# Splitting weights by chunks of four channel blocks in three 4 KB tiles, instead of by two blocks in six 2 KB tiles

## The chip, the cores and the metric

The kernel runs on one core of a Trainium2 chip. A core has five engines with queues of their own, each working through its instructions in the order in which the program issues them: TensorE (matmuls; PE in the profile, its weight loads PEld), VectorE (DVE), ScalarE (ACT), GpSimd (POOL) and SyncE (SP, which here issues all DMAs). SBUF is the on-chip memory of 128 partitions; a tile of "4 KB" has 4 KB in each partition. Matmuls write to PSUM banks of 128 x 512 float32.

The metric is the time of one execution on the device in microseconds. Three runs of the kernel before gave 1795.52, 1795.69 and 1798.46 us; the median is 1795.69.

## The reference

One layer over 1024 tokens and 2048 channels, in float32:

```python
hn = rmsnorm(h, norm_gain)
proj = hn @ w_in                       # 2048 x 4096
pool_in, pool_gate, ssm_in, ssm_gate = four column blocks of 1024
ya = pool_mixer(pool_in, w_pool, pool_scale) * silu(pool_gate)
yb = ssm_mixer(ssm_in, ...) * silu(ssm_gate)
h = h + concatenate([ya, yb]) @ w_out  # 2048 x 2048
h = h + (p @ w_ple) * sigmoid(h @ w_ple_gate)
return rmsnorm(h, final_gain)
```

`pool_mixer` takes trailing means over windows of 2, 4, 8 and 16 tokens and a 256 x 256 product for each of four channel groups. `ssm_mixer` is a state-space layer: 64 groups of 16 channels share 64 complex states each; its output passes GELU and a gated linear unit with the 1024 x 2048 weight `w_glu`.

## The kernel before, in words

**Products in two parts.** TensorE multiplies a reduced form of float32 (`F32R` in the code). To keep precision, each operand is split into a high part (rounded to that form) and a low part (the rest), and three products are summed: high x high, high x low, low x high. For weights this split is done on the fly, each time a weight chunk arrives: ScalarE writes the high part (`act.copy`, a CAST in the profile, L199), VectorE subtracts it from the raw chunk for the low part (a TENSOR_TENSOR w<-raw,w in the profile; all such operations pass the helper at L96).

**Chunks and steps.** The dense work is a list of `chunks` (weights loaded by one DMA) and a list of `steps` (what TensorE does with a part of a chunk). A chunk of the usual kind is 128 output channels by four channel blocks of 128 (256 KB, tile `raw`, of which there are three, `r_p`). A narrow step takes two channel blocks (`kk` = 0 or 2 of the chunk) for one or both halves of 512 tokens: 2 blocks x 3 products = 6 matmuls of 128 x 512 with one half, 12 with both. Chunks of only two blocks, with one step each, occur in the first stage (steps 0 to 7, 24 to 39 and 56 to 63, when x is still arriving; steps 8 to 23 and 40 to 55 use chunks of four blocks) and in the products of the pooling branch (eight steps in all). There are 568 narrow steps from 304 chunks. Steps 0 to 63 have 6 matmuls each, steps 64 and on have 12 until near 785 us. At the end of the kernel wide steps take one channel block by 512 columns as the moving operand; there are 128 of them with a chunk of their own.

**The split before.** `split(s)` (L189) makes the split weights of one step. A narrow step gets one tile of `w_p` with 2 x 2 x 128 float32 (2 KB): cast and subtraction of 256 columns. A wide step gets two such tiles, one for the high and one for the low part (`split_wide`, L203): cast and subtraction of 512 columns. `w_p` has `NW` = 6 tiles.

**The order.** The order of all engines is written out by hand. `emit(s)` (L245) issues for step s, in this order: loads whose raw tile is free (`emit_loads`, L237: the load of chunk c is issued after the last split of chunk c-3 has been issued), stores held back, then splits of coming steps, as far as step s + `SA` (`SA` = 4) and as long as the steps from s on together hold no more than `NW` tiles (`nw`: one for a narrow step, two for a wide one, L153 and L161); then the `pre` work of the step, the background generators (`bg`), the matmuls (`run_mats`, L210) and the `post` work. So on ScalarE and VectorE the split for step s+4 stands ahead of the other work of step s. A new tile in a place that an old one had waits until all that read the old one are done.

**Work around it.** In the first stage, `x_proc` (L310) turns pieces of x on TensorE, ScalarE copies them out (`xt`, L318) and VectorE splits them (`hn`, L321 and L322); ScalarE also sums squares (L336); `u_raw` (L396) and `u_scale` (L402) work on outputs on VectorE. From step 40 on the state-space branch runs in the background, one piece for each 2.56 us of matmul work counted: `ss_prep`, then `ss_b` and `ss_l` side by side, `ss_v`, `ss_scan`, `ss_y`. `ss_b` (L603) builds a tile `m` in three VectorE operations (L613 to L615) in one piece, and the next piece turns it on TensorE (L621) ahead of that step's matmuls and copies it out on ScalarE (L623). `ss_scan` (L780) is a chain of VectorE operations on 128 x 64 elements with larger ones on GpSimd between; `ss_y` (L805) begins with a mask on GpSimd (`ytm`, L825). The windows of the pooling branch (`pool_win`, L916) run in the background later, on GpSimd, VectorE and ScalarE.

Of the kernel before, what the change touches and what calls it, by code (L numbers as in the profile page):

```python
# [17 lines left out]
L = 1024          # tokens  # L18
HT = 512          # tokens per half
D = 2048  # L20
KD = D // P       # 16 channel blocks of the model
W = 1024          # width of a branch
KW = W // P       # 8 channel blocks of a branch
G = 64            # state-space groups
N = 64            # states of a group
C = 16            # channels of a group
T = 8             # tokens of a chunk of the scan
NC = L // T       # chunks
# [7 lines left out]
NW = 6            # tiles of split weights  # L36
# [3 lines left out]
def hybrid_trunk(ctx: ExitStack, tc: tile.TileContext, x, p, norm_gain, w_in, w_pool, pool_scale,  # L40
# [33 lines left out]
    g_d = dr.tile([W, T, NC], F32, name="g_d")            # t descending  # L74
# [6 lines left out]
    K_d = dr.tile([G * C * P + P], F32, name="K_d")       # overlapping rows, see ss_y  # L81
# [25 lines left out]
    # ------------------------------------------------------------ constants  # L107
# [7 lines left out]
    sgn = cst.tile([P, 2], F32, name="sgn")     # [:,0] -1 | +1, [:,1] +1 | -1  # L115
# [12 lines left out]
    dT = cst.tile([64, 16], F32, name="dT")      # of (four groups, c), by four groups  # L128
    same = cst.tile([64, C], F32, name="same")   # of (g ci), co: ci = co
    parT = cst.tile([P, 24], F32, name="parT")  # L130
    mask = cst.tile([P, T], F32, name="mask")   # of (ci ti), to: ti + to < T
# [9 lines left out]
    # ------------------------------------------------------------ dense steps  # L141
# [3 lines left out]
    def chunk(ap, nk):  # L145
        chunks.append({"ap": ap, "nk": nk, "raw": None, "last": None})
        return len(chunks) - 1

    def step(ch, kk, mats, pre=(), post=()):
        """mats: list of (bank key, activation getters of two channel blocks, start, stop)"""  # L150
        chunks[ch]["last"] = len(steps)
        steps.append({"ch": ch, "kk": kk, "mats": mats, "pre": list(pre), "post": list(post),
                      "w": None, "nw": 1, "dur": 1.28 * len(mats)})  # L153

    def wide_step(ch, mats, post=()):
        """tokens on partitions; mats: list of (bank key, bank pool, activation getter, columns,
        weights or None for those of the chunk, start, stop)"""
        if ch is not None:
            chunks[ch]["last"] = len(steps)
        steps.append({"ch": ch, "kk": None, "mats": mats, "pre": [], "post": list(post),  # L160
                      "w": None, "nw": 0 if ch is None else 2, "dur": 0.64 * len(mats)})  # L161
# [8 lines left out]
    def store(o, i, n=1):  # L170
        """a store on the queue of the loads, held back so that it does not wait there"""
        late.append([n, o, i])
# [16 lines left out]
    def split(s):  # L189
        sd = steps[s]  # L190
        if sd["ch"] is None:
            return
        if sd["kk"] is None:
            raw = chunks[sd["ch"]]["raw"].rearrange("p a c -> p (a c)")
            sd["w"] = split_wide(raw)
            return
        raw = chunks[sd["ch"]]["raw"][:, sd["kk"]:sd["kk"] + 2]
        w = w_p.tile([P, 2, 2, P], F32R, tag="w", name="w")
        act.copy(out=w[:, 0], in_=raw)  # L199
        tt(dve, w[:, 1], raw, f(w[:, 0]), ALU.subtract)  # L200
        sd["w"] = w

    def split_wide(raw):  # L203
        hi, lo = (w_p.tile([P, 2, 2, P], F32R, tag="w", name="w").rearrange(
            "p a b c -> p (a b c)") for _ in range(2))
# [4 lines left out]
    def run_mats(s):  # L210
        sd = steps[s]
        w = sd["w"]
# [14 lines left out]
        for i in range(2):  # L227
            for j, (wi, ai) in enumerate(((0, 0), (0, 1), (1, 0))):
                for key, ks, start, stop in sd["mats"]:
                    a = acts[ks[i]]  # L230
                    pe.matmul(out=banks[key], lhsT=w[:, wi, i], rhs=a[:, ai],  # L231
                              start=start and i == 0 and j == 0, stop=stop and i == 1 and j == 2)

    SA = 4
# [10 lines left out]
    def emit(s):  # L245
        emit_loads()
        emit_stores()
        while (state["split"] <= min(s + SA, len(steps) - 1)
               and sum(d["nw"] for d in steps[s:state["split"] + 1]) <= NW):
# [19 lines left out]
        sd["w"] = None  # L269

    def block(wap, ks, halves, akey, bkey, post):
        """One block of 128 output channels over the given channel blocks and token halves."""
# [1176 lines left out]
```

## Time and profile before

| | |
|---|---|
| three runs, median | 1795.69 us |
| lowest, highest | 1795.52, 1798.46 us |
| span of the profiled execution | 1795.3 us |
| DVE idle before w<-raw,w of 256 columns, waiting for the cast | 333.4 us of 335.6 |
| ACT idle before the cast of 256 columns, waiting for matmuls | 449.8 us of 531.6 |
| HBM read, written | 178.63 MB, 55.05 MB |

The time of the profiled execution as a whole isn't recorded beside its span; the span, from its first to its last instruction, is 0.4 us below the median of the three runs. Busy time of an engine is the time in which one of its instructions ran. In rows of a timeline the first number is the start in microseconds from the start of the span, the second how long the row lasts, "xN" how many instructions of the same kind it merges; in square brackets stand the idle time of the engine ahead of the row and what ended it. In a group of instructions the numbers after the bar are busy time in us, mean ns of one instruction, and idle time of the engine ahead of them. Instructions of one engine overlap at their ends, so from the start of one to the start of the next may be less than the duration. In tables of stretches the bounds are followed by the length, then the busy time of each engine, the granted clock of TensorE (1.00 is full speed), the share of the DMA engines and GB/s.

### The profile page before, as it was taken

The numbers are of one execution on the slowest core, as the hardware profiler recorded it, in microseconds if no ns is written. First come the engines' busy times: TensorE is split into PE (matmuls) and PEld (weight loads), VectorE is DVE, ScalarE is ACT, GpSimd is POOL, SyncE is SP. The second block draws the span as 40 slices with busy tenths as digits, with TensorE's granted clock in tenths as the row PEclk, the third lists the DMA queues.
The fourth block names the chain that finished last, engine by engine and source line by source line (L and its number), as shares of the span: only waits on it lengthen the run. The fifth ranks groups of instructions, "written<-read, shape, count | busy, mean of one in ns | idle before, by whom it ended". The sixth has DMA issues, their size and how long they took to land.

```text
span 1795.3 us, 23117 instructions
## 1 busy us (share of the span) xinstructions
PE 1748.6 (97%) x8054; PEld 1444.8 (80%) x8054; DVE 975.2 (54%) x1792; ACT 613.2 (34%) x1389; POOL 370.3 (21%) x395
## 2 busy tenths in 40 slices
PE   8999899999989999999999999999999999999998
PEld 7888678887768888887888888888888888777787
DVE  5755987479985745447533442222245554466542
ACT  6641355341124522126322231111133333344332
POOL 0065143024341114204011100000001211233320
PEclk9999999999989999999999999999999999999999
DMA  8853333542246622247532353333365333363312
GB/s 264 240 167 94 126 119 125 169 126 71 65 129 188 205 83 82 83 126 191 170 112 76 93 184 106 94 96 98 100 194 194 120 114 124 113 208 117 120 59 94
DMA packets 299510, 235.21 MB, mean 131 GB/s; under 512 B 51689, under 2 KB 242178, under 8 KB 298498
## 3 DMA queue, kind: packets, MB, share of 16 engines
q1 hardware_dynamic: 299394, 233.75, 42.0%
q8 instruction: 63, 1.03, 0.2%
q14 instruction: 53, 0.43, 0.1%
HBM read 178.63 MB, written 55.05 MB: 130 GB/s over the span
## 4 chain that ended last, share of the span: by engine, by line
PE 80%; DVE 10%; issue 3%; POOL 3%; ACT 2%; DMA 1%; SPq 0%; ACTq 0%; POOLq 0%; DVEq 0%
PE mm L231 58%; PE mm L221 16%; DVE w L96 2%; PE aux L221 2%; DVE V L96 2%; POOL nat L96 2%; DVE V L756 1%; ACT V L758 1%; POOL pf L96 1%; PE aux L867 1%; PE bk L1184 1%; PE aux L865 1%; DVE m L96 1%; DVE tB L96 1%; PE aux L316 1%
## 5 line engine op out<-in xcount | busy, mean ns | idle before, releaser
L231 PE MATMUL mm<-hn,w 128*128 128x512 f32 x3072 | 725.2, 393 | 7.5 <-DVE w L96 6.0
L231 PEld LDWEIGHTS mm<-hn,w 128*128 128x128 f32 x3072 | 573.4, 189 | 129.8 <-DVE w L96 10.0
L96 DVE TENSOR_TENSOR w<-raw,w 128x256 fp32r<-128x256 f32 (+1 forms) x696 | 391.6, 578 | 502.9 <-ACT w L199 333.4
L199 ACT CAST w<-raw 128x256 fp32r<-128x256 f32 x568 | 222.4, 407 | 531.6 <-PE mm L231 449.8
L221 PE MATMUL mm<-w,h 128*128 128x512 f32 x1359 | 320.1, 392 | 6.1 <-DVE w L96 6.1
L221 PEld LDWEIGHTS mm<-w,h 128*128 128x128 f32 x1359 | 252.2, 188 | 60.2 <-DVE w L96 9.1
L231 PE MATMUL mm<-g,w 128*128 128x512 f32 x768 | 176.5, 390 | 3.2 <-DVE w L96 2.8
L231 PE MATMUL mm<-yb,w 128*128 128x512 f32 x768 | 177.9, 389 | 0.0
L231 PEld LDWEIGHTS mm<-g,w 128*128 128x128 f32 x768 | 143.5, 188 | 36.0 <-DVE w L96 5.7
L231 PEld LDWEIGHTS mm<-yb,w 128*128 128x128 f32 x768 | 144.1, 188 | 29.9
L206 ACT CAST w<-raw 128x512 fp32r<-128x512 f32 x128 | 79.3, 620 | 210.9 <-PE mm L221 153.6
L96 POOL TENSOR_TENSOR hs<-h 128x512 f32<-128x512 f32 x32 | 52.0, 1651 | 377.0 <-DVE h L96 340.8
L231 PE MATMUL mm<-yaq,w 128*128 128x512 f32 x384 | 127.2, 389 | 0.0
L231 PE MATMUL mm<-ya,w 128*128 128x512 f32 x384 | 127.0, 389 | 0.0
L96 POOL TENSOR_TENSOR nat<-nat,fg 128x512 f32<-128x512 f32 x28 | 45.9, 1668 | 246.7 <-ACT sig L1210 219.0
L231 PEld LDWEIGHTS mm<-ya,w 128*128 128x128 f32 x384 | 72.1, 188 | 15.0
L231 PEld LDWEIGHTS mm<-yaq,w 128*128 128x128 f32 x384 | 72.0, 188 | 14.9
L96 POOL TENSOR_TENSOR pf<-pf 128x1023 f32<-128x1023 f32 (+7 forms) x28 | 50.1, 1789 | 161.1 <-DVE pf L96 152.6
L96 DVE TENSOR_TENSOR xtl<-mm,xtl 128x512 f32<-128x512 f32 x32 | 21.1, 687 | 56.1 <-PE mm L231 53.9
L96 POOL TENSOR_TENSOR sb<-sb,sgt 128x512 f32<-128x512 f32 x16 | 21.9, 1389 | 138.8 <-ACT sb L1018 138.8
L379 ACT ACTIVATE gs<-mm 128x512 f32<-128x512 f32 x32 | 18.8, 599 | 87.9 <-DVE mm L96 87.8
L96 POOL TENSOR_TENSOR t<-V,AR 128x512 f32<-128x512 f32 (+2 forms) x13 | 16.9, 1300 | 149.0 <-ACT V L758 84.8
(197 smaller groups left out, 1603.2 us busy)
## 6 DMA issues: line engine op xcount, KB each, us to landing
raw<-in_w_in_dram SPq DMA_DIRECT2D x136, 256.0 KB, 2.9
raw<-in_w_ple_gate_dram SPq DMA_DIRECT2D x112, 256.0 KB, 3.2
raw<-in_w_out_dram SPq DMA_DIRECT2D x88, 256.0 KB, 2.8
raw<-in_w_glu_dram SPq DMA_DIRECT2D x40, 256.0 KB, 2.8
xT_d<-xt SPq DMA_DIRECT2D x32, 256.0 KB, 3.8
xtl<-xT_d SPq DMA_DIRECT2D x32, 256.0 KB, 3.6
h_d<-xtl SPq DMA_DIRECT2D x32, 256.0 KB, 2.1
hl<-h_d SPq DMA_DIRECT2D x32, 256.0 KB, 4.0
```

The lines of the kernel that those rows point to most:

```text
L96: eng.tensor_tensor(out=o, in0=a, in1=b, op=op)
L199: act.copy(out=w[:, 0], in_=raw)
L206: act.copy(out=hi, in_=raw)
L221: pe.matmul(out=banks[key][:, part], lhsT=a[:, ai, cols], rhs=b[:, part], start=start and j == 0, stop=stop and j == 2)
L231: pe.matmul(out=banks[key], lhsT=w[:, wi, i], rhs=a[:, ai], start=start and i == 0 and j == 0, stop=stop and i == 1 and j == 2)
L316: pe.transpose(b[:, i * P:(i + 1) * P], xr[:, i], ident)
L379: act.activation(out=s, in_=b, func=AF.Sigmoid)
L756: dve.tensor_copy(out=o.rearrange("p k c -> p c k"), in_=i)
L758: act.copy(out=o.rearrange("p k c -> p c k"), in_=i)
L865: pe.matmul(out=o, lhsT=ttl[:, i * P:(i + 1) * P], rhs=ut[:, i * P:(i + 1) * P], start=True, stop=False)
L867: pe.matmul(out=o, lhsT=lt[:, i * P:(i + 1) * P], rhs=sv[:, i * P:(i + 1) * P], start=False, stop=True)
L1184: pe.transpose(fin["b"][tb][:, (k % 4) * P:(k % 4 + 1) * P], hs[:, tb * P:(tb + 1) * P], ident)
```

## The change

Narrow steps no longer have split weights of their own. The first step of a chunk makes the split of the whole chunk (up to four blocks, 512 columns: one cast, one subtraction) into one tile of 2 x 4 x 128 float32 (4 KB); the second step of the chunk finds it made. `w_p` has three such tiles in place of six of half the size, so it takes the same 12 KB. A wide step uses one tile, with the high part in its first half and the low part in its second. A chunk of two blocks takes a tile too, and fills half of it. `SA` is 5 in place of 4, and the bound on the splits ahead is now that steps s to the one to be split use at most three different chunks. The tile is let go after the last step of its chunk. The matmuls are the same, in the same order. (Comments are dropped as well.)

```diff
-NW = 6            # tiles of split weights
+NW = 3
...
     def split(s):
-        sd = steps[s]
-        if sd["ch"] is None:
+
+        c = steps[s]["ch"]
+        if c is None or chunks[c]["w"] is not None:
             return
-        if sd["kk"] is None:
-            raw = chunks[sd["ch"]]["raw"].rearrange("p a c -> p (a c)")
-            sd["w"] = split_wide(raw)
+        ch = chunks[c]
+        if steps[s]["kk"] is None:
+            ch["w"] = split_wide(ch["raw"].rearrange("p a c -> p (a c)"))
             return
-        raw = chunks[sd["ch"]]["raw"][:, sd["kk"]:sd["kk"] + 2]
-        w = w_p.tile([P, 2, 2, P], F32R, tag="w", name="w")
-        act.copy(out=w[:, 0], in_=raw)
-        tt(dve, w[:, 1], raw, f(w[:, 0]), ALU.subtract)
-        sd["w"] = w
+        nk = ch["nk"]
+        raw = ch["raw"][:, 0:nk]
+        w = w_p.tile([P, 2, 4, P], F32R, tag="w", name="w")
+        act.copy(out=w[:, 0, 0:nk], in_=raw)
+        tt(dve, w[:, 1, 0:nk], raw, f(w[:, 0, 0:nk]), ALU.subtract)
+        ch["w"] = w
 
     def split_wide(raw):
-        hi, lo = (w_p.tile([P, 2, 2, P], F32R, tag="w", name="w").rearrange(
-            "p a b c -> p (a b c)") for _ in range(2))
+        w = w_p.tile([P, 2, 4, P], F32R, tag="w", name="w")
+        hi, lo = (w[:, i].rearrange("p b c -> p (b c)") for i in range(2))
         act.copy(out=hi, in_=raw)
         tt(dve, lo, raw, f(hi), ALU.subtract)
         return hi, lo
...
     def run_mats(s):
         sd = steps[s]
-        w = sd["w"]
+        w = None if sd["ch"] is None else chunks[sd["ch"]]["w"]
...
-                    pe.matmul(out=banks[key], lhsT=w[:, wi, i], rhs=a[:, ai],
+                    pe.matmul(out=banks[key], lhsT=w[:, wi, sd["kk"] + i], rhs=a[:, ai],
...
-    SA = 4
+    SA = 5
...
         while (state["split"] <= min(s + SA, len(steps) - 1)
-               and sum(d["nw"] for d in steps[s:state["split"] + 1]) <= NW):
+               and len({d["ch"] for d in steps[s:state["split"] + 1]} - {None}) <= NW):
...
-        sd["w"] = None
+        if sd["ch"] is not None and sd["ch"] not in {d["ch"] for d in steps[s + 1:s + 20]}:
+            chunks[sd["ch"]]["w"] = chunks[sd["ch"]]["raw"] = None
```

More of the change, by code (lines that the diff above doesn't have):

```diff
@@ L145, in chunk @@
     def chunk(ap, nk):
-        chunks.append({"ap": ap, "nk": nk, "raw": None, "last": None})
+        chunks.append({"ap": ap, "nk": nk, "raw": None, "w": None, "last": None})
         return len(chunks) - 1
@@ L152, in step @@
         steps.append({"ch": ch, "kk": kk, "mats": mats, "pre": list(pre), "post": list(post),
-                      "w": None, "nw": 1, "dur": 1.28 * len(mats)})
+                      "w": None, "dur": 1.28 * len(mats)})
     def wide_step(ch, mats, post=()):
@@ L160, in wide_step @@
         steps.append({"ch": ch, "kk": None, "mats": mats, "pre": [], "post": list(post),
-                      "w": None, "nw": 0 if ch is None else 2, "dur": 0.64 * len(mats)})
+                      "w": None, "dur": 0.64 * len(mats)})
     acts = {}
```

## The prediction

> **What bounds the kernel now.** I read the page first (span, engines, chain), then the busy times by stretches, then the groups of the split, then single rows where TensorE stands still.
>
> ```profile
> span 1795.3 us, 23117 instructions
> ...
> PE 1748.6 (97%) x8054; PEld 1444.8 (80%) x8054; DVE 975.2 (54%) x1792; ACT 613.2 (34%) x1389; POOL 370.3 (21%) x395
> ...
> PE 80%; DVE 10%; issue 3%; POOL 3%; ACT 2%; DMA 1%; SPq 0%; ACTq 0%; POOLq 0%; DVEq 0%
> ```
>
> TensorE is busy for 1748.6 of 1795.3 us. The change leaves every matmul as it is, so at most the other 46.7 us can be won, and time is lost only where TensorE comes to wait. The stretches show where it waits already.
>
> ```profile
> core 0: us, PE busy (x) PEld busy (x) DVE busy (x) ACT busy (x) POOL busy (x), PEclk, DMA share, GB/s
> 0.00:60.00 60.00, 54.22 (x261) 44.67 (x262) 35.10 (x81) 39.62 (x125) 3.22 (x37) 1.00 0.79 250
> 58.00:79.00 21.00, 20.29 (x106) 16.89 (x105) 20.75 (x40) 14.96 (x51) 0.00 (x0) 1.00 0.81 240
> 60.00:110.00 50.00, 49.29 (x253) 40.52 (x251) 37.21 (x73) 32.74 (x110) 12.55 (x28) 1.00 0.81 230
> ...
> 165.00:235.00 70.00, 59.84 (x298) 47.88 (x297) 67.46 (x89) 21.00 (x42) 10.20 (x8) 1.00 0.43 132
> 235.00:390.00 155.00, 155.00 (x749) 130.46 (x748) 101.39 (x192) 78.39 (x166) 31.85 (x25) 1.00 0.46 143
> 390.00:430.00 40.00, 36.99 (x159) 29.28 (x158) 38.52 (x63) 8.12 (x21) 24.21 (x16) 1.00 0.19 60
> 430.00:530.00 100.00, 91.63 (x389) 73.59 (x388) 96.33 (x292) 18.61 (x47) 43.66 (x37) 0.96 0.25 78
> 508.00:512.00 4.00, 2.19 (x10) 1.51 (x9) 3.97 (x6) 0.00 (x0) 3.90 (x3) 1.00 0.01 2
> 512.00:514.00 2.00, 2.00 (x7) 1.53 (x6) 1.90 (x12) 0.10 (x1) 0.00 (x0) 0.50 0.88 300
> 820.00:860.00 40.00, 36.76 (x154) 27.99 (x153) 30.80 (x49) 22.41 (x41) 20.41 (x14) 1.00 0.56 144
> 860.00:1367.00 507.00, 507.00 (x2243) 419.82 (x2242) 173.21 (x341) 128.38 (x306) 24.51 (x18) 1.00 0.40 126
> ```
>
> In 235 to 390 and 860 to 1367 TensorE has no idle time at all. In 165 to 235 (B and L of the state-space branch are built) VectorE is 96% busy and TensorE idles 10.2 us; in 390 to 530 (the scan) VectorE is 96% busy again and TensorE idles 11.4 us. Until 110 us VectorE (74%) and the DMA engines (81%) are nearly full. These three places decide.
>
> **The change part by part.**
>
> *Fewer, longer instructions.* The groups of the split, kept apart by shape:
>
> ```profile
> L96 DVE TENSOR_TENSOR w<-raw,w 128x256 fp32r<-128x256 f32 x568 | 271.9, 496 | 335.6 <-ACT w L199 333.4
> L199 ACT CAST w<-raw 128x256 fp32r<-128x256 f32 x568 | 222.4, 407 | 531.6 <-PE mm L231 449.8 <-DMA raw<-in_w_in_dram 40.4 <-DVE w L96 11.2
> L206 ACT CAST w<-raw 128x512 fp32r<-128x512 f32 x128 | 79.3, 620 | 210.9 <-PE mm L221 153.6 <-DMA raw<-in_w_ple_gate_dram 31.4 <-PE aux L221 19.6
> ```
>
> Of the 568 narrow steps 40 stay alone (32 of the first 64, 8 of the pool products), 528 become 264 pairs. Two casts of 407 ns become one of 620, off the path. On VectorE the duration isn't the price, since instructions overlap:
>
> ```profile
> 202.54 0.69 DVE L96 TENSOR_TENSOR m<-m,mw 128x512 f32<-128x512 f32 x1
> 203.16 0.42 DVE L96 TENSOR_TENSOR w<-raw,w 128x256 fp32r<-128x256 f32 x1
> 203.49 1.17 DVE L96 TENSOR_TENSOR m<-qb,qa 128x512 f32<-128x512 f32 x1
> ```
>
> A 512-column subtraction holds VectorE for 0.62 us until the next start, a 256-column one for 0.33, so a pair saves 2 x 0.33 - 0.62 = 0.04 us (by durations 0.15). That counts only where VectorE is full. By counting matmuls (64 steps of 6, then 12 each), 165 to 235 emits about 9 pairs and 390 to 530 about 21: 30 x 0.04 = 1.2 us, at most 30 x 0.15 = 4.5.
>
> The Trainium skill, Perfetto Trace Analysis, section Optimizing Scalar/DVE Operations, puts the overhead of a DVE instruction on SBUF at about 60 ns; an estimate from it is 30 x 0.06 = 1.8 us, and the trace's 0.04 nearly agrees. The same section says that where these engines aren't saturated but cause bubbles elsewhere, breaking instructions up may let work finish sooner; that speaks against this change, and the next parts price it from rows.
>
> *When a split may start.* Before, step k took the tile that step k-6 had left: in steady stretches its cast begins as step k-6 ends on TensorE. After, the pair (k, k+1) takes the tile of (k-6, k-5), so its cast waits for the end of k-5, which in program order is the step just before the one that emits it. With two token halves the lead shrinks by one step of 12 matmuls, from about five steps to four: hidden by the matmuls of those four. In 235 to 390, 530 to 820 and 860 to 1367 I cost it at nothing. Loads are emitted one step earlier relative to use there, also nothing. Wide steps held two 2 KB tiles each, three steps at a time; now one of 4 KB, three at a time: nothing.
>
> *B and L, 165 to 235.* Here the cover fails. VectorE computes m in three instructions in step s, behind the subtraction emitted in that step, and TensorE turns m at the start of step s+1.
>
> ```profile
> 165.18 1.12 DVE L96 TENSOR_TENSOR m<-qb,qa 128x512 f32<-128x512 f32 x1
> 166.12 1.16 DVE L96 TENSOR_TENSOR mw<-qb,qa 128x512 f32<-128x512 f32 x1
> 167.31 0.69 DVE L96 TENSOR_TENSOR m<-m,mw 128x512 f32<-128x512 f32 x1
> ```
> ```profile
> 167.11 0.41 ACT L199 CAST w<-raw 128x256 fp32r<-128x256 f32 x1 [2.31 <-PE mm L231]
> ```
> ```profile
> 169.64 0.60 PE L621 MATMUL aux<-ident,m 128*128 128x128 f32 x4
> 169.99 3.02 PE L231 MATMUL mm<-hn,w 128*128 128x512 f32 x12
> 172.85 0.60 PE L621 MATMUL aux<-ident,m 128*128 128x128 f32 x4
> ...
> 191.62 0.63 PE L621 MATMUL aux<-ident,m 128*128 128x128 f32 x4 [1.33 <-DVE m L96]
> ```
>
> By the same count the row at 169.99 is step 83, and the cast at 167.11 starts as step 81 ends. The first m is that of step 82. After, step 82 emits the split of steps 86 and 87, which waits for the end of 81: cast 167.11 to 167.73, subtraction to 168.39, m 2.8 us later at 171.2. TensorE wanted it at 169.64: 1.6 us lost. The loop goes on: from the end of a step, cast (0.62), subtraction (0.62), m (2.8) make 4.1 us, but TensorE's step lasts 3.2 (169.64 to 172.85), so each even step loses up to 0.9; m of the odd step needs no split and lets TensorE catch part of it, VectorE's other work makes up the rest. Carried on by hand, TensorE is 2.2 us late at step 85, 2.9 at 87, 3.4 at 89 (195.0 for 191.62) and between 3.3 and 4.0 from there, where VectorE no longer waits. I take +3.7; at least 0 (VectorE had that slack), at most 5.
>
> *Steps 0 to 63.* Steps with a chunk of two blocks (0 to 7, 24 to 39, 56 to 63) use a whole 4 KB tile each: three steps may be split at a time, so a split is emitted two steps ahead, not four. Each step is 6 matmuls, 1.36 us. VectorE's queue at the worst place:
>
> ```profile
> 73.80 0.43 DVE L96 TENSOR_TENSOR w<-raw,w 128x256 fp32r<-128x256 f32 x1
> ...
> 76.51 1.14 DVE L96 TENSOR_TENSOR u<-u,rstd 128x512 f32<-128x512 f32 x1
> 77.56 2.11 DVE L96 TENSOR_TENSOR w<-raw,w 128x256 fp32r<-128x256 f32 x6
> ```
> ```profile
> 69.80 7.53 PE L231 MATMUL mm<-hn,w 128*128 128x512 f32 x32
> 78.04 2.57 PE L231 MATMUL mm<-hn,w 128*128 128x512 f32 x10 [0.71 <-DVE w L96]
> ```
>
> The subtractions at 73.80 and 77.56 are emitted by steps 35 and 36; now they serve steps 39 and 40, after the change 37 and 38. The row of 32 matmuls begins with step 35, so step 38 starts 18 matmuls later, 73.9, and needs its low part two matmuls on, 74.4. VectorE, busy 20.75 of 21 us from 58 to 79, delivers at 77.1 (if two subtractions fewer ahead of it help by 0.66) to 78.0: a wait of 2.7 to 3.6 in place of 0.71. Net +2.3, between 0 and 2.9. The first chunk of four blocks (steps 8, 9) is loaded only once step 5 is split.
>
> ```profile
> 13.19 1.16 DVE L96 TENSOR_TENSOR w<-raw,w 128x256 fp32r<-128x256 f32 x3 [2.42 <-ACT w L199]
> ```
> ```profile
> 21.84 0.71 ACT L199 CAST w<-raw 128x256 fp32r<-128x256 f32 x2 [1.35 <-DMA raw<-in_w_in_dram]
> ```
> ```profile
> 15.41 1.63 PE L231 MATMUL mm<-hn,w 128*128 128x512 f32 x6
> ...
> 24.93 1.43 PE L231 MATMUL mm<-hn,w 128*128 128x512 f32 x5
> ```
>
> Step 5 is the last of the three subtractions at 13.19 and is done at 14.35. After, its tile is that of step 2, whose matmuls (row 15.41) end at 17.0: done 17.9 at the earliest, 3.5 later. The cast of steps 8 and 9 waits for its load and starts at 21.84; later by up to 3.5, it starts at 25.3, and step 8 wanted it done at 24.93: 25.3 + 0.62 - 24.93 = 1.0. Some of the 3.5 may be slack in the load queue: +0.8, between 0 and 2 (the same again for the next chunk). For steps 56 to 64, which lose the same two steps of lead, TensorE shows no second wait in 60 to 110 now (0.71 us in all); no row gives their slack, +0.4, between 0 and 1.
>
> *The scan, 390 to 530.* TensorE resumes when VectorE's chain and the mask behind it are through:
>
> ```profile
> 527.76 0.80 PE L865 MATMUL aux<-yu,ytm 128*128 128x128 f32 x2 [4.96 <-POOL ytm L96]
> ```
>
> So only a shorter chain helps: 21 pairs x 0.04 = 0.9 us, at most 21 x 0.15 = 3. Waits for a single split on the way shift, but don't move that end. I take -1.0. At 820 to 860 TensorE idles 3.2 us with GpSimd half busy, and I take the chain there to be alike: -0.3, between -1 and +0.5.
>
> **Sum.** +3.7 + 2.3 + 0.8 + 0.4 - 1.0 - 0.3 = +5.9 us on a span of 1795.3, which lies 0.4 below the median 1795.69 of the three runs (what lies around the span, kept as it is): 1801.6, said as 1801.5. The ends add up to -4.0 (0 + 0 + 0 + 0 - 3 - 1) and +11.4 (5 + 2.9 + 2 + 1 + 0 + 0.5).
>
> **The rivals.** *Shorter VectorE work wins.* In the two full stretches each pair saves its 0.15 of duration, 30 x 0.15 = 4.5, and the new waits hide in slack: 1791. It decides if VectorE at 165 to 175 is so late that the end of the step before is always past. For it: VectorE is 96% full there. Against it: the row at 167.11 shows ScalarE idle for 2.31 us waiting for TensorE, so VectorE is not late when m begins. Chance 0.12.
>
> *The cover holds.* The lead lost is taken from slack nearly everywhere, only one or two of the four places cost: 1795.7 + 1 to 3, 1797.5. For it: TensorE waits only 0.71 us in 60 to 110, so the early steps have slack to give. Against it: the two chains above were followed row by row. Chance 0.25.
>
> *TensorE's clock falls too.* In 508 to 512 TensorE stood still for 1.8 us, and in 512 to 514 its granted clock is 0.50. The mean of 0.96 over 430 to 530 is 0.04 x 100 = 4 us of work lost; I take it for two falls of 2 us. If the wait of 2.7 at step 38 and one in 165 to 235 each bring such a fall, that is 4 more: 1805.5. Against it: the wait of 1.33 at 191.62 brought none, the clock of 165 to 235 being 1.00. Chance 0.13. The Trainium skill, TensorE: Matmul & The Clock Gate, Part 1, gives half rate after an idle window of about 3.4 us; the rate agrees with the row, but here 1.8 us idle within 4 were enough.
>
> **How the numbers follow.** The forecast has 0.50, the rivals 0.12, 0.25 and 0.13. A measurement of this kernel tells some 0.2% (3.6 us) from no change. Slower by more: 0.45 of the forecast, the falling clock's 0.13, 0.05 of the held cover: 0.63. Within: the other 0.05 and 0.20: 0.25. Faster: 0.12. The range from 1794 to 1807 takes in the cover that holds and the falling clock and leaves out the shorter work and the upper end of the bounds.
>
> **What would show it.** Casts of 128x512 in 264 places, each starting as the step before the emitting one ends; TensorE's idle time in 165 to 235 up from 10.2 to about 14 us, with VectorE idle behind "ACT w"; a wait of 2 to 3 us for the split near 74 to 78 us in place of 0.71, and one near 25 us; no idle time in 860 to 1367. I am wrong if VectorE isn't held by casts at 165 to 190, or if the subtractions of steps 37 and 38 are ready in time, or if the scan ends more than 3 us sooner.

## The result and the profile after

| | before | after |
|---|---|---|
| median of the runs compared, us | 1796.83 (4 runs) | 1809.57 (4 runs, 1808.53 to 1810.51) |
| ratio, 95% interval | | 1.0070 (1.0056 to 1.0084) |
| second comparison, us | 1797.83 (15 runs) | 1814.04 (5 runs, 1809.92 to 1815.02) |
| ratio, 95% interval | | 1.0082 (1.0069 to 1.0096) |
| span of the profiled execution, us | 1795.3 | 1807.7 (second: 1813.0) |

The change makes the kernel slower by 12.7 us, or 0.7%; I had forecast slower by 5.9 us, and the time lies above my range (1794 to 1807). The page of the changed kernel begins so:

```profile
span 1807.7 us, 22311 instructions
...
PE 1752.7 (97%) x8054; PEld 1444.5 (80%) x8054; DVE 931.0 (51%) x1528; ACT 577.1 (32%) x1125; POOL 375.2 (21%) x395
...
PE 76%; DVE 12%; issue 3%; DMA 3%; POOL 2%; ACT 2%; SPq 1%; ACTq 0%; POOLq 0%; DVEq 0%
...
L96 DVE TENSOR_TENSOR w<-raw,w 128x512 fp32r<-128x512 f32 (+1 forms) x432 | 334.3, 778 | 594.3 <-ACT w L201 422.2
L201 ACT CAST w<-raw 128x512 fp32r<-128x512 f32 (+1 forms) x304 | 179.2, 593 | 585.1 <-PE mm L233 501.8
```

The change does what it says: 264 casts and 264 subtractions fewer, VectorE 44 us and ScalarE 36 us less busy (931.0 for 975.2, 577.1 for 613.2). TensorE gained nothing by it: its idle time rises from 46.7 to 55.0 us (1807.7 - 1752.7). Its busy time rises too, by 4.1 us with the same 8054 matmuls. Some 1.2 us of that lie where the clock is low; it stood at 0.50 for 10.2 us in each of the two profiles, before in part while TensorE waited. Most of the rest stands at the waits. In steady rows a matmul lasts 0.39 us and the next starts 0.23 us after it; a wait ends this overlap, so TensorE falls behind by 0.16 us more than the idle time ahead of the row says (1.59 us at the wait of 1.44 at 178.76, 0.41 at one of 0.25).

TensorE executes the same instructions in the same order in both kernels, so the k-th can be compared with the k-th. I call the difference of their starts how far TensorE is *behind*. Read at the limits of the stages, it says where time is lost; negative numbers are gains. The stages are named by the time of the kernel before, and the last row is the difference of the spans.

| stage | predicted | first profile after | second profile after |
|---|---|---|---|
| steps 0 to 63 (to 140 us) | +3.5 | +7.5 | +9.6 |
| transforms B and L (165 to 300) | +3.7 | +5.2 | +6.7 |
| scan (390 to 560) | -1.0 | -4.2 | -2.1 |
| 820 to 870 | -0.3 | +2.7 | +2.3 |
| wide steps (1367 to the end) | 0 | +1.1 | +1.2 |
| span | +5.9 | +12.4 | +17.7 |

Small differences between the rows and the sum are drift of a few tenths. A second profile of the kernel before differs from the first by at most 0.2 us at these limits, and by 1.7 us for a moment within the scan, where a fall of the clock at 512 us is missing. But a first stage whose code was left alone came out between 0.7 us ahead and 2.3 us behind in the runs below, so single profiles decide nothing of that size there.

**Steps 0 to 63.** The waits of TensorE for the low part of the weights (us in all, how many, the longest) in the changed kernel from 0 to 110 us, where before had one of 0.7; then rows of the changed kernel:

```profile
PE mm L233 <- DVE w L96: 5.5, 6, 2.0
```
```profile
32.74 0.62 ACT L201 CAST w<-raw 128x512 fp32r<-128x512 f32 x1 [1.60 <-DMA raw<-in_w_in_dram]
...
37.21 1.15 ACT L201 CAST w<-raw 128x512 fp32r<-128x512 f32 x2
...
39.99 1.20 PE L233 MATMUL mm<-hn,w 128*128 128x512 f32 x4 [1.36 <-DVE w L96]
```
```profile
78.44 1.07 DVE L96 TENSOR_TENSOR u<-u,rstd 128x512 f32<-128x512 f32 x1
79.43 0.76 DVE L96 TENSOR_TENSOR w<-raw,w 128x256 fp32r<-128x256 f32 x2
79.90 3.55 PE L233 MATMUL mm<-hn,w 128*128 128x512 f32 x9 [2.04 <-DVE w L96]
```

The rows of the timeline show two of the six. At 79.90 is the wait that I predicted at step 38, with its cause: the low part comes right behind VectorE's work on u. At 39.99 is one that I didn't see (step 16). Its history starts at the cast of steps 14 and 15, at 32.74, which waited for its weights to arrive. What stands behind it in ScalarE's queue comes late too: copies of x, and then the cast of steps 16 and 17 at 37.21. Before, the casts of step 14 and of steps 16 and 17 started at 28.33 and 32.90:

```profile
28.33 0.41 ACT L199 CAST w<-raw 128x256 fp32r<-128x256 f32 x1 [0.25 <-DMA raw<-in_w_in_dram]
...
32.90 0.72 ACT L199 CAST w<-raw 128x256 fp32r<-128x256 f32 x2
```

Smaller waits stand near 22 us (0.39), 61 (0.44), 76 (0.23) and 99 (1.03). After the wait at 79.90 the granted clock falls (windows of 2 us, the clock is the third number from the end):

```profile
80.00:82.00 2.00, 2.00 (x7) 1.58 (x8) 0.88 (x2) 0.62 (x1) 0.00 (x0) 0.68 0.44 120
82.00:84.00 2.00, 2.00 (x6) 1.62 (x5) 0.53 (x1) 0.62 (x1) 0.00 (x0) 0.50 1.02 342
```

Read by place, TensorE falls behind by 0.4 at 22 us, 1.8 at 40, 0.7 at 61, 0.6 at 76, 2.3 at 80, 1.7 by the slow clock behind it, and 1.1 at 99; it wins back the 0.9 of the wait at 78.04 that is now gone.

**Transforms.** Waits of TensorE from 165 to 250 us in the changed kernel (10.2 us in 8 waits before), and the first pair of the stage, the end of whose step 81 lies at 174.60 by the single matmuls of the trace:

```profile
PE aux L624 <- DVE m L96: 14.0, 15, 2.3
```
```profile
174.64 0.62 ACT L201 CAST w<-raw 128x512 fp32r<-128x512 f32 x1 [4.82 <-PE mm L233]
...
175.29 0.69 DVE L96 TENSOR_TENSOR w<-raw,w 128x512 fp32r<-128x512 f32 x1 [2.95 <-ACT w L201]
...
178.76 0.66 PE L624 MATMUL aux<-ident,m 128*128 128x128 f32 x4 [1.44 <-DVE m L96]
```

This is the chain of the prediction, row by row: the cast starts as the step before the emitting one ends, VectorE stands idle for it for 2.95 us, and m, three operations behind, comes 1.44 us late. From the cast to TensorE's work on m it is 4.1 us, as forecast.

**820 to 870.** A wait for a cast grew from 0.37 us to 1.48, and the clock fell behind it:

```profile
864.60 5.64 PE L233 MATMUL mm<-g,w 128*128 128x512 f32 x15 [1.48 <-ACT w L201]
```
```profile
866.00:868.00 2.00, 2.00 (x6) 1.54 (x6) 1.97 (x2) 0.37 (x2) 1.53 (x1) 0.50 0.29 85
```

**Scan.** TensorE restarts with less wait than before (4.96 us):

```profile
538.21 0.49 PE L868 MATMUL aux<-yu,ytm 128*128 128x128 f32 x2 [1.95 <-POOL ytm L96]
```

### The profile page after: what moved, and what is told of

It is laid out like the page before. It is cut to its first block, busy times and chain, and to the rows that moved or that the text cites. A ratio compares the mean times of both kernels' runs of the same rounds, so it can differ in the third digit from the quotient of the medians.

```text
span 1807.7 us, 22311 instructions
## 1 busy us (share of the span) xinstructions
PE 1752.7 (97%) x8054; PEld 1444.5 (80%) x8054; DVE 931.0 (51%) x1528; ACT 577.1 (32%) x1125; POOL 375.2 (21%) x395
## 3 DMA queue, kind: packets, MB, share of 16 engines
q8 instruction: 63, 1.03, 0.2%
## 4 chain that ended last, share of the span: by engine, by line
PE 76%; DVE 12%; issue 3%; DMA 3%; POOL 2%; ACT 2%; SPq 1%; ACTq 0%; POOLq 0%; DVEq 0%
PE mm L233 54%; PE mm L223 16%; DVE w L96 3%; DVE V L96 2%; PE aux L223 2%; DMA raw<-in_w_in_dram 2%; DVE m L96 1%; DVE tA L96 1%; DVE tB L96 1%; PE bk L1187 1%; PE aux L870 1%; PE aux L868 1%; PE aux L749 1%; DVE mw L96 1%; DVE sig L96 1%
## 5 line engine op out<-in xcount | busy, mean ns | idle before, releaser
L96 DVE TENSOR_TENSOR w<-raw,w 128x512 fp32r<-128x512 f32 (+1 forms) x432 | 334.3, 778 | 594.3 <-ACT w L201 422.2
L201 ACT CAST w<-raw 128x512 fp32r<-128x512 f32 (+1 forms) x304 | 179.2, 593 | 585.1 <-PE mm L233 501.8
```

Source lines behind the costliest of these rows:

```text
L96: eng.tensor_tensor(out=o, in0=a, in1=b, op=op)
L201: act.copy(out=w[:, 0, 0:nk], in_=raw)
```

## The experiments

All runs are compared with the kernel before on the same chip (its medians lay between 1797.8 and 1798.3 us). "Transforms", "scan" and so on are stages as in the table above. The intervals in the headings are those of the ratio.

### The lead of the early steps

The lead is how many steps ahead of its matmuls a split is issued. **e3_before_short_lead**: 1805.1 us, 1.0038 (1.0023 to 1.0053). The kernel before; a chunk of two blocks counts as two tiles, so that only three steps fit.

```diff
-               and sum(d["nw"] for d in steps[s:state["split"] + 1]) <= NW):
+               and sum(
+                   2 if d["nw"] == 1 and chunks[d["ch"]]["nk"] == 2 else d["nw"]
+                   for d in steps[s:state["split"] + 1]) <= NW):
```

> The kernel before, splits by two blocks, but the chunks of two blocks are split only two steps ahead instead of four; nothing else is changed. Theory (the lost lead alone costs the early 7.4 us, its clock fall among them): TensorE is 5 to 8 us later by the end of step 63 and the time is about 1803. Rival (the lead had slack to give, the bursts cost): 1797 to 1798.

TensorE is 7.8 us behind by the end of step 63, and the time is up by 7.2 us, with every split as short as before. Its row at step 38, and its clock behind it, are those of the changed kernel:

```profile
80.04 3.48 PE L231 MATMUL mm<-hn,w 128*128 128x512 f32 x10 [2.03 <-DVE w L96]
```
```profile
82.00:84.00 2.00, 2.00 (x6) 1.57 (x5) 0.65 (x2) 0.71 (x2) 0.00 (x0) 0.50 1.00 344
```

**e1_small_tiles**: 1798.6 us, 1.0002 (0.9993 to 1.0012). The change, with the lead given back.

```diff
-NW = 3
+NW = 6
...
-        w = w_p.tile([P, 2, 4, P], F32R, tag="w", name="w")
...
+        if nk == 2:
+            w = w_p.tile([P, 2, 2, P], F32R, tag="w", name="w")
+            hi, lo = w[:, 0], w[:, 1]
+        else:
+            hi, lo = (w_p.tile([P, 2, 2, P], F32R, tag="w", name="w").rearrange(
+                "p a b c -> p (a b) c") for _ in range(2))
...
-    SA = 5
+    SA = 4
...
-               and len({d["ch"] for d in steps[s:state["split"] + 1]} - {None}) <= NW):
+               and sum(1 if chunks[c]["nk"] == 2 else 2 for c in {d["ch"] for d in steps[
+                   s:state["split"] + 1]} - {None}) <= NW):
```

> Chunks are still split whole, but from six tiles of 2 KB: a chunk of two blocks takes one and is split four steps ahead again, a chunk of four takes two. Theory (the lead that the two-block chunks lost costs the 7.4 us which TensorE is behind by the end of step 63): that falls to 1 us or less, and the time to about 1803. Rival (it is the longer subtraction of the four-block chunks, in bursts, that keeps VectorE's queue late): 1808 or more. In the stage of the B and L transforms both expect the same 5 us loss as with the change.

The early loss falls from 7.5 to 1.6 us. But the time falls by 11 us, not by the 6.6 expected, because other stages change as well: the transforms lose 2.1 instead of 5.2, and the wide steps nothing instead of 1.1. Two tiles instead of one matter elsewhere too.

**e7_lead_first8** (1801.0 us, 1.0015, 1.0006 to 1.0024) and **e8_lead_24_39** (1801.1 us, 1.0016, 1.0006 to 1.0025) shorten the lead in one of the two groups of steps; the edit is that of e3 with the condition `k < 8` or `24 <= k < 40`.

> The kernel before, with the splits of steps 0 to 7 alone two steps ahead instead of four. Theory (later splits free the load buffers later; the loads of the chunks behind come late, and their casts run into ScalarE's work on x): TensorE waits 1 to 2.5 us near step 16 (39 us), nothing at steps 37 and 38; time about 1800. Rival (the lead of the first eight steps is slack; the early loss comes all from steps 24 to 39): 1797 to 1798.

> The kernel before, with the splits of steps 24 to 39 alone two steps ahead instead of four. Theory (the subtractions of steps 37 and 38 come behind VectorE's work for u and hn): a wait of 2 to 3 us near step 38, a granted clock of 0.50 for some 3 us right behind it, in all 4 to 5.5 us lost by step 63, time about 1802. Rival (this wait stands only because the loads were already late from the first eight steps): 1798 or less.

```profile
39.83 2.34 PE L231 MATMUL mm<-hn,w 128*128 128x512 f32 x9 [0.97 <-DVE w L96]
```
```profile
77.58 3.03 PE L231 MATMUL mm<-hn,w 128*128 128x512 f32 x7 [2.03 <-DVE w L96]
```

The first row is of e7, the second of e8. Each group has its own wait, step 16 for the first and step 38 for the second, and each costs 3.3 us by the medians (1.1 to 4.5 by the intervals); together 6.6 of the 7.2. The loads that come late belong to the first eight steps: a load is issued only after the split of the third chunk before it, so a shorter lead of the splits is a shorter lead of the loads. e8 also brought the slow clock (0.50 from 78 to 80 us).

### The transforms

**e2_one_later**: 1805.8 us, 1.0040 (1.0025 to 1.0055). The changed kernel, one number changed.

```diff
-    SA = 5
+    SA = 3
```

> The change with SA = 3: a chunk of four blocks is split by the second step of a pair instead of the first of the next, so that its cast waits for a step that ended a whole step earlier; the work is the same. Theory (in the stage of the transforms the cast's wait holds VectorE's subtraction, and m stands behind it): the loss of 5.3 us there falls to 1 or below, the time to about 1804.5, and TensorE's wait for m is as before the change. Rival (a longer piece of VectorE work in front of m costs it wherever it stands): 1809, loss unchanged. The first 64 steps, limited by their tiles, should lose the same 7 us in both.

The loss in the transforms is gone (7.4 us behind ahead of them, 7.1 after), with subtractions just as long, and the waits for m are down to those of before:

```profile
PE aux L624 <- DVE m L96: 9.7, 8, 1.8
```

The Trainium skill, Perfetto Trace Analysis, section Optimizing Scalar/DVE Operations, says that where these engines aren't saturated but cause bubbles elsewhere, breaking instructions up may let work finish sooner. Here the trace doesn't bear it out: the long subtraction cost nothing once its cast waited for an earlier step, and e14, below, breaks the subtractions up again and loses 4.8 us.

**e6_transforms_only**: 1800.1 us, 1.0010 (1.0001 to 1.0019). The kernel before, with whole-chunk splits only in some steps, from the two tiles of e1. The same edit with other limits makes e5, e9, e15 and e16.

```diff
+    def whole(s):
+        return steps[s]["kk"] is None or chunks[steps[s]["ch"]]["nk"] == 4 and 64 <= s < 112
...
-        nk = ch["nk"]
-        raw = ch["raw"][:, 0:nk]
+        nk = ch["nk"] if whole(s) else 2
+        raw = ch["raw"][:, 0:nk] if whole(s) else ch["raw"][:, steps[s]["kk"]:steps[s]["kk"] + 2]
```

> The kernel before, with whole-chunk splits only in steps 64 to 111 (the B and L transforms); all else by two blocks. Theory (the cast that waits for the end of the step before it holds VectorE ahead of m): TensorE is 2 to 5 us later by the end of the transforms, with its loss at the first six m, and the time is 1800 to 1802. Rival (the loss there follows only from the late start that the first 64 steps hand on): 1797 to 1798.

2.1 us are lost in the transforms: the theory's mechanism, but not the 5.2 of the change. **e10_lead_and_transforms** (1806.7 us, 1.0052, 1.0039 to 1.0064) adds the short lead of e3:

> The kernel before, with the two-block chunks split only two steps ahead and whole-chunk splits in steps 64 to 111; all else by two blocks, six tiles of 2 KB. Theory (the two losses add up: 7.2 us for the lead, 2.3 for the transforms): 1807 to 1808. Rival (in the transforms the late start makes the loss larger, 5.3 us as in the changed kernel): 1810 to 1811.

The losses add up; the late start is not what makes the 5.2. What is left is the tile. By the single matmuls, the cast of the first pair starts 0.04 us after the end of step 81 in the changed kernel, and 0.42 us before it in e1, e6 and e10: with separate tiles it waits only for the matmuls that read the high part, and the last two of a step read the low part.

**e11_swapped_tiles** (1799.6 us, 1.0007, 0.9998 to 1.0016) and **e12_glu_swapped** (1798.5 us, 1.0005, 0.9996 to 1.0013) were to undo that by swapping the two tiles of every other chunk (`hi, lo = lo, hi`).

> As the run with whole-chunk splits only in the transforms (steps 64 to 111), but every other chunk takes its two 2 KB tiles the other way round, so that the high part overwrites the tile that held the low part three chunks before, which the last two matmuls of the step read. Theory (with one 4 KB tile the cast waits for those two matmuls too, 0.45 us longer at every pair, and this is what makes the loss in the transforms 5.2 us instead of 2.1): the cast starts 0.04 us after the end of the step instead of 0.42 before it, TensorE is 4.5 to 5.5 us later by the end of the transforms, and the time is 3 us above the run without the swap, about 1803. Rival (the 4 KB tile or the late start cost it in another way): 2 us later and 1800 as without the swap.

> As the run with whole-chunk splits only in steps 276 to 327, with the tiles taken the other way round at every other chunk. Theory (the later end of the cast's wait is what costs there): TensorE 2 to 3 us later by 870 us, a fall of the granted clock near 860 among it, and 1800 to 1801. Rival: 1 us or less, 1798 to 1799, as without the swap.

They answered nothing: in e11 the cast still starts 0.42 us before the end of step 81. I take it that the place of a tile is chosen when it is first written, and the high part is always written first; no run shows it. What they give is a repeat of e6 and of e9. So I put the parts into one tile by another way.

**e13_one_tile** (1813.8 us, 1.0076, 1.0062 to 1.0090) and **e14_halves_one_tile** (1812.9 us, 1.0080, 1.0067 to 1.0094): the changed kernel with its three tiles of 4 KB, but each step fills its own half of the tile; e13 splits whole chunks in the transforms alone, e14 nowhere in the narrow steps.

```diff
-        if c is None or chunks[c]["w"] is not None:
+        whole = steps[s]["kk"] is None or 64 <= s < 112
+        if c is None or chunks[c]["w"] is not None and whole:
...
+        if ch["w"] is None:
+            ch["w"] = w_p.tile([P, 2, 4, P], F32R, tag="w", name="w")
+        w, kk = ch["w"], steps[s]["kk"]
+        r = slice(0, ch["nk"]) if whole else slice(kk, kk + 2)
+        act.copy(out=w[:, 0, r], in_=ch["raw"][:, r])
+        tt(dve, w[:, 1, r], ch["raw"][:, r], f(w[:, 0, r]), ALU.subtract)
```

> The changed kernel with its three tiles of 4 KB, but only steps 64 to 111 (the transforms) split a chunk whole; elsewhere each step splits its own two blocks into its half of the chunk's tile. Beside the run with six tiles of 2 KB, short lead and whole-chunk splits in the same steps (1806.7, loss in the transforms 1.9 us). Theory (in one tile the cast waits for the last two matmuls too, 0.45 us longer at every pair): the cast starts 0.04 us after the end of a step instead of 0.42 before it, the loss between 165 and 235 us is 4.5 to 5.5, and the time about 1810. Rival (the 5.2 us come from the state in which the first 64 steps leave the queues): 2 us and 1807.

> The changed kernel with its three tiles of 4 KB, but every step splits its own two blocks into its half of the chunk's tile: tiles, lead and waits for tiles as with the change, lengths of the work as before it. Theory (waits, not lengths, cost in the transforms: of two halves only the first waits for the end of a step, but VectorE is held by it as well): a loss of 2 to 4 us there, between none and that of the whole chunk; 7 us in the first 64 steps; nothing gained in the scan, so 1808 to 1811. Rival (the length of the piece in front of m costs): no loss in the transforms, 1805.

First the cast and the first m of e10 (separate tiles, step 81 ends at 174.09), then those of e13 (one tile, step 81 ends at 175.44):

```profile
173.67 0.62 ACT L217 CAST w<-raw 128x512 fp32r<-128x512 f32 x1 [4.82 <-PE mm L252]
...
177.81 0.66 PE L644 MATMUL aux<-ident,m 128*128 128x128 f32 x4 [1.01 <-DVE m L96]
```
```profile
175.48 0.62 ACT L203 CAST w<-raw 128x512 fp32r<-128x512 f32 x1 [4.82 <-PE mm L234]
...
179.60 0.66 PE L625 MATMUL aux<-ident,m 128*128 128x128 f32 x4 [1.43 <-DVE m L96]
```

The wait is longer by 0.42 at the first pair, and by 0.46 at the second: the transforms lose 5.0 us in e13 against 1.9 in e10. e13's time is nonetheless 3.8 us above the expected 1810; its profile has the clock at 0.50 for 17.1 us against 10.2 before, which is 3.4 us of lost work (the fall near 241 us, within the transforms, adds nothing to the 5.0: the wait behind it shrank to 0.25 us, where the changed kernel has 1.88). e14 loses 4.8 in the transforms, more than the 2 to 4 expected. In its trace both halves of a chunk are split together (`x2`), since five steps of lead reach the second half in the step that splits the first, so VectorE is held as by the whole chunk. So it isn't the width of the split that costs. e14's time, 14.6 us above before, shows that the tiles and the lead alone make the kernel as slow as the change does.

**e4_small_later** (1798.9 us, 1.0004, 0.9994 to 1.0013) takes the tiles of e1 and splits pairs three steps ahead:

> Both mends at once: six tiles of 2 KB, two-block chunks four steps ahead, four-block chunks split three steps ahead by the second step of a pair. Theory: early loss 1 or less, loss in the transforms 1 or less, and what the change gained in the scan (4 us) stays: 1794 to 1797, level with the kernel before or a little below. Rival (the whole-chunk work itself costs): 1803 or more.

Early loss 1.2 us, transforms -0.3: both mends hold. The gain in the scan did not stay, though, so the time missed the 1794 to 1797; with three steps of lead TensorE falls behind by up to 10.6 us in the scan (11.7 in e2), and catches it up at its end but for 0.9 in e2.

### The scan

**e5_scan_only**: 1794.8 us, 0.9980 (0.9972 to 0.9989). As e6, with `112 <= s < 224`.

> The kernel before, with whole-chunk splits only in steps 112 to 223 (around the scan of the chunk states, six tiles of 2 KB, lead as before); all else by two blocks. Theory (in that stretch TensorE waits for VectorE's chain, and the fewer, longer subtractions shorten it by some 6 us, 22.6 in 29 for 28.8 in 57): TensorE gains 3 to 4 us there and loses nothing elsewhere, 1794 to 1795. Rival (the gain in the changed kernel was only TensorE catching up after it had come late): 1797 to 1798.

The time is the theory's, the reason is not. VectorE's last operation on V starts 0.7 us *later* against TensorE's start of the stage than before, in the changed kernel and in e5. The gain has its place in SyncE's queue and on GpSimd. Before:

```profile
515.54 7.17 SPq L187 DMA_DIRECT2D raw<-in_w_in_dram  x2
...
521.89 2.16 DVE L96 TENSOR_TENSOR w<-raw,w 128x256 fp32r<-128x256 f32 x3
522.80 0.46 SPq L814 DMA_DIRECT2D yt<-K_d  x1
...
526.57 1.13 POOL L96 TENSOR_TENSOR ytm<-yt,mask 128x512 f32<-128x512 f32 x1 [3.14 <-DMA yt<-K_d]
```

After:

```profile
527.09 4.03 SPq L187 DMA_DIRECT2D raw<-in_w_in_dram  x2
...
531.21 0.46 SPq L817 DMA_DIRECT2D yt<-K_d  x1
...
537.05 1.11 POOL L96 TENSOR_TENSOR ytm<-yt,mask 128x512 f32<-128x512 f32 x1
```

The rows of SPq are issues of DMAs; SyncE issues them one after the other. Before, the second load of weights stands in the queue until the second half of the chunk of steps 192 and 193 has been subtracted, at 522.3, behind the last work on V. The load of yt stands behind it, and GpSimd waits 3.14 us for it ahead of the mask, and TensorE for GpSimd. After, that chunk is read by one subtraction, the load goes, yt is there, and GpSimd goes on without a wait. Two runs put this to the test: **e15_one_chunk** (1794.6 us, 0.9981, 0.9972 to 0.9990) splits that one chunk whole (`192 <= s < 194`), **e16_scan_before_it** (1798.9 us, 1.0004, 0.9995 to 1.0013) all of the stretch ahead of it (`112 <= s < 192`).

> The kernel before, with one single chunk split whole, that of steps 192 and 193; all else by two blocks. Theory (before, the second subtraction of this chunk stands behind the end of VectorE's chain, until 522.3 us; the next load of weights waits for it in SyncE's queue, and behind that load stands the one of yt, for which GpSimd waits 3.1 us; one subtraction for the chunk lets both loads go some microseconds sooner): GpSimd's wait for yt goes, TensorE restarts 1.5 to 2.5 us sooner than before, 1795.5 to 1796.5. Rival (the gain comes from VectorE's shorter chain over the whole stretch, as I predicted it and wrote for the run of the scan alone): one pair saves 0.1 us or nothing, 1797.5 to 1798.5.

> The kernel before, with whole-chunk splits in steps 112 to 191, not in 192 and 193. Theory (the load of yt decides at the end of the scan): GpSimd still waits some 3 us for yt, TensorE restarts within 0.7 us of before, 1797 to 1798.5. Rival (VectorE's shorter chain): 2 to 3 us gained as in the run of the scan alone, 1795.

e15, then e16:

```profile
515.93 2.44 SPq L187 DMA_DIRECT2D raw<-in_w_in_dram  x2
...
518.47 0.46 SPq L837 DMA_DIRECT2D yt<-K_d  x1
...
524.01 1.29 POOL L96 TENSOR_TENSOR ytm<-yt,mask 128x512 f32<-128x512 f32 x1
```
```profile
516.70 8.73 SPq L187 DMA_DIRECT2D raw<-in_w_in_dram  x2
...
525.53 0.46 SPq L837 DMA_DIRECT2D yt<-K_d  x1
...
528.88 1.12 POOL L96 TENSOR_TENSOR ytm<-yt,mask 128x512 f32<-128x512 f32 x1 [2.73 <-DMA yt<-K_d]
```

One pair of casts and subtractions made into one gains 3.4 us by the medians (1.8 to 5.0 by the interval), more than the 1.5 to 2.5 expected; the forty pairs ahead of it gain nothing. Nor does the pair have to become one instruction. e14 merges none, and I expected nothing in the scan; it gained 3.2 us there, 1.3 of them by TensorE's restart. It issues both halves of the chunk in one step, ahead of the last work on V, and so the load goes, yt is there, and GpSimd has no wait:

```profile
532.18 0.76 DVE L96 TENSOR_TENSOR w<-raw,w 128x256 fp32r<-128x256 f32 x2
...
533.44 0.46 SPq L818 DMA_DIRECT2D yt<-K_d  x1
...
539.02 1.29 POOL L96 TENSOR_TENSOR ytm<-yt,mask 128x512 f32<-128x512 f32 x1
```

What counts, by these runs, is when the second half is subtracted. e15 and e5, 0.2 us apart, are the fastest kernels of this study, and faster than both kernels compared.

### Later stages

**e9_glu_only**: 1799.0 us, 1.0004 (0.9995 to 1.0013). As e6, with `276 <= s < 328`.

> The kernel before, with whole-chunk splits only in steps 276 to 327 (short steps of six matmuls, 780 to 870 us); all else by two blocks. Theory (the cast of a pair waits for the end of the step before, and its split stands ahead of ScalarE's and VectorE's other work there): TensorE loses 1 to 2.5 us by 870 us, a fall of the granted clock among it, and the time is 1799 to 1800. Rival (the loss there came only with the shifted start): 1797 to 1798.

By 870 us it lost 0.4 us, and its repeat e12 0.5, though e12 has a wait of 1.52 us for the cast where the changed kernel has one of 1.48. No clock fell there, nor in e2, e4 and e14, which lose 1.1, 0.2 and 0.4. In e1, e13 and both profiles of the changed kernel a fall of 3.4 us to half clock lies between 856 and 876 us, and those lose 2.0 to 2.8; 1.7 of that is the fall. So the loss of this stage is mostly the clock, and what makes it fall there in one execution and not in another was not tried.

The wide steps lose 1.1 to 1.3 us in the changed kernel, its repeat and e2, all with one 4 KB tile, and nothing in e1 and e4 with two of 2 KB (e13 and e14, one tile, lose 2.5 and 1.8). The waits for the low part, from 1367 us to the end, first the changed kernel, then e1:

```profile
PE mm L223 <- DVE w L96: 7.4, 7, 1.4
```
```profile
PE mm L228 <- DVE w L96: 6.1, 7, 1.2
```

Seven waits as before (6.1 us), six of them longer by 0.22, about what one matmul takes from start to start there (25 in 5.83 us before). That one tile comes free a matmul later is what this fits; no run changed the wide tile alone.

**r_after** and **r_before** repeat the two kernels for second profiles. The numbers of r_after stand in the tables above; r_before is one run, 1797.2 us.

> The changed kernel once more, for a second profile and beside the runs above: 1809.6, TensorE 7 to 8 us behind by the end of step 63 and 12 to 13 us by the end of the transforms if that stage's 5.3 us belong to the program; some 10 us by then if they vary from one execution to the next.

> The kernel before once more, for a second profile: the start of each matmul within 1 us of the first profile; where it differs by more, a loss read from two profiles is no surer than that difference.

The transforms lost 6.7 us in the repeat, but one fall of the clock near 247 us, 1.7 us, is in that. The loss there belongs to the program, and it is a fall more or less that varies. r_before kept to within 1 us but for the 1.7 in the scan named above.

## Why the prediction was right and wrong

*Direction, and "fewer, longer instructions".* The direction was right: VectorE's 44 us brought nothing, and the rival of the shorter work (1791) did not come about. In the stages that I costed at nothing, 235 to 390, 530 to 820 and 860 to 1367, nothing was lost (the wait and the fall near 866 us apart). One reading was loose: VectorE's 74% "until 110 us" is that of 60 to 110; from 0 to 110 it is 66% (72.3 us).

*Steps 0 to 63, +3.5, measured 7.5.* This step failed most. The wait at step 38 was right in place and cause, and nearly in size: 2.04 us and 0.23 just ahead of it, where I had 2.7 to 3.6. What failed is "The first chunk of four blocks (steps 8, 9) is loaded only once step 5 is split", followed no further than step 8: there it cost 0.4 instead of 0.8, but the late loads went on into steps 14 to 16 and cost 1.8 at 40 us, and waits near 61 and 99 us, which I didn't price at all, came with the lost lead. For steps 56 to 64 I wrote +0.4, and nothing was lost there. The rival of the falling clock, which I gave 0.13, came true behind step 38 (1.7 us), not in 165 to 235 of the first profile. e3 shows 7.2 us for the lead alone, e7 and e8 3.3 for each group.

*B and L, +3.7, measured 5.2.* The mechanism was right, as e2 shows by taking it away; the size was not. I wrote that TensorE's idle time there would rise from 10.2 to about 14 us, and the waits sum to 14.0. But I took the idle time for the whole loss: there are 15 waits instead of 8, and each new one costs 0.16 us beyond its idle time, 1.1 of the missing 1.5. That the sum came to 14.0 is partly luck. The carrying by hand held to step 89 (3.4 late predicted, 3.7 measured, with the 0.16 of five waits in it). What failed is "between 3.3 and 4.0 from there, where VectorE no longer waits": two later pairs cost another 1.1 and 0.8 us of wait, of which the other waits behind step 89 gave back 0.8. And in the expectation of e1 I took it as given that two tiles would make the same wait as one; e10 and e13 put 3 of the 5 us on the parts sharing a tile.

*Scan, -1.0, measured -4.2 and -2.1.* The sign was right by luck, the mechanism wrong: "So only a shorter chain helps". The chain did not get shorter; a load got out of another's way. 2.2 us of the 4.2 are there when TensorE restarts (1.8 against the second profile of before); the rest is a clock that was slow over 526 to 532 us before and had recovered by the restart after. In the second profile after it was slow there again, and the gain was 2.1. Without this gain the miss would have been larger by 3.2 us.

*820 to 860, -0.3, measured +2.7.* I took this stage to be like the scan. It is a cast that waits, which costs 1.0 us here and 0.2 to 1.1 in the runs without a fall, and then a fall of the clock, 1.7.

*Wide steps, 0, measured +1.1.* That it would still be "three at a time" was right, but a tile that holds both parts seems to come free later than the first of two.

## What to carry to other kernels

When buffers are merged, count what the merging does to the lead (a half-filled tile is a whole one to the allocator, and loads hang on the splits) and to the wait (a tile comes free with the last reader of either part); the saving in instructions counts only where somebody waits for that engine. When a gain shows up, look for its place as hard as for a loss: 3.4 us hung on one chunk that held a load queue; the other 263 merged pairs were not needed for it, and by e14 not even this one, only an earlier subtraction of its second half.

## What the hardware did that I had not expected

A short stop of TensorE can cost as much again by the clock, and not always. In the two profiles of the changed kernel the same matmul waited 2.10 us (at 501.32) and 2.03 us (at 504.83). First the windows behind it in the first profile, then in the second:

```profile
503.00:505.00 2.00, 2.00 (x10) 1.63 (x10) 1.90 (x10) 0.00 (x0) 0.00 (x0) 1.00 0.27 76
```
```profile
506.00:508.00 2.00, 2.00 (x7) 1.57 (x6) 1.86 (x10) 0.00 (x0) 0.00 (x0) 0.56 0.45 130
508.00:510.00 2.00, 2.00 (x7) 1.56 (x6) 1.93 (x7) 0.00 (x0) 0.85 (x1) 0.59 0.13 36
```

In the second profile the clock is short of full by 0.44 and 0.41 of 2 us each, which makes 1.7 us of lost work. All in all the clock stood at 0.50 for 10.2 us in the first profile and for 20.5 in the second; that is 5.1 us of lost work more, and the spans differ by 5.3. So the same program varies by several us from run to run: 1809.92 to 1815.02 in the second comparison.

The Trainium skill, TensorE: Matmul & The Clock Gate, Part 1, puts the clock at half rate after an idle window of about 3.4 us, and calls this window free-running. The falls here agree in depth and length: 0.50, for 3.4 us or twice that. But one came after a stop of 2.04 us, at 79.90, which is shorter than that window, and the measurement decides. Whether a stop counts may depend on where in the window it lies; no run here shows it.
